# Hybrid flow backbone step on one core: the SSD's PSUM tiles in turn from two tags, and an earlier place for one part of the output projection

## The chip, the cores and the metric

The kernel runs on one core of one Trainium2 chip. The metric is device time in microseconds (us) of a whole execution; the number for a kernel is the median of its runs. PE is the matmul engine, ACT the scalar engine, DVE the vector engine, POOL the GpSimd engine, SP the engine from whose queue all DMA transfers of this kernel are issued.

## The reference, cut to what matters

Two layers work on 128 prompt tokens and 512 sample tokens of 1024 features. Each layer has a mixer with four groups of heads side by side, whose outputs are joined and projected, then a gated feed-forward net (FFN). Scales, shifts and gates come from a modulation of the conditioning vectors (adaLN).

```python
def trunk_layer(x, mod, P, layer_idx, ctx):
    h = rmsnorm(x, P['g_pre1']) * (1.0 + scale1) + shift1
    ...
    ya = diff_attention(a_q, a_k, a_v, lam)
    ...
    yb = gqa_attention(b_q, b_k, b_v).reshape(b, L, W_B)
    ...
    y = jnp.concatenate([ya, yb, yc.astype(ya.dtype), yd.astype(ya.dtype)], axis=-1) @ P['w_out']
    x = x + gate1 * rmsnorm(y, P['g_post1'])
    h = rmsnorm(x, P['g_pre2']) * (1.0 + scale2) + shift2
    ...

def ssd_scan(x, dt, A, Bm, Cm, h0):
    ...
    decay = jnp.where(mask, jnp.exp(jnp.where(mask, seg, 0.0)), 0.0)
    gmat = jnp.einsum('btlhn,btshn->btlsh', Cc, Bc) * decay
    y_diag = jnp.einsum('btlsh,btshp->btlhp', gmat, xc)
    decay_to_end = jnp.exp(a_cum[:, :, -1:, :] - a_cum)
    chunk_states = jnp.einsum('btshn,btsh,btshp->bthpn', Bc, decay_to_end, xc)
    chunk_decay = jnp.exp(a_cum[:, :, -1, :])
    ...
    y_off = jnp.einsum('btlhn,bthpn,btlh->btlhp', Cc, h_enter, jnp.exp(a_cum))
    return (y_diag + y_off).reshape(b, L, h, p), h_final
```

The mixer's 1024 output features are 8 chunks of 128: 0 to 3 come from the two attentions, 4 and 5 from the SSD (a state space model with scalar decays), 6 and 7 from the S5 mixer.

## The kernel before, in words

Everything is kept with features on the 128 partitions and 642 columns of tokens, split into two groups of columns (256 and 386, `SPANS`). Large matmuls run in three passes over a high and a low part of both operands (`lin3`, L124), so that each weight tile of 128x1024 is loaded (`wr`), cast on ACT to its high part (`wh`, L103) and subtracted on DVE or POOL in turn to its low part (`wl`, L106). Pool `wp` holds two buffers each of `wr`, `wh` and `wl` for all streamed weights of the kernel; in layer 0 the modulation's weights (`wm`, L234) use the same two `wr` buffers.

A scheduler orders the instructions at compile time. Each instruction has a priority (lower goes first), which counts up by one per instruction from the number given to `prio(...)` (L1428); the numbers are in `PR` and `WP` (L42, L43). Each engine then executes its own list in that order, and waits in it for its operands. Tiles of one pool and tag share the tag's buffers.

PSUM has eight banks: tag p two, e two, d two, v one, u one (`pss`, L157). The projections, the head norms, the modulation of layer 0 and the output projection take p (the latter's last part p and e in turn); the S5 mixer, its gated output and the whole SSD take d; attention takes e, u and v.

The mixer (`mixer`, L1438) writes a layer's work down in this order, each part with its priority relative to the layer's base: input projections and key and query preparation (40000), the SSD's step sizes (`ssd_steps`, 55000, one p tile), the S5 mixer (0), in layer 0 modulation group 1 (`fill(0)`, 60000, two p tiles), the S5 gated output (10000), the SSD (30000), attention (35000), the output projection over chunks 6 and 7 (61000), in layer 0 modulation group 2 (`fill(1)`, 61000, two p tiles), the output projection over chunks 0 and 1 (62000; the weights' chunks are stored in the order 0, 2, 1, 3, so these are the first unit of each attention). Then come the norms (300000), with the output projection over the other four chunks for one group of columns after the other, and the FFN (320000). The first input weights of layer 1 have the priority 321000 (L470).

```python
1488              with self.pool(f"sd{l}", "right") as sd, self.prio(base + PR["ssd"]):
1489                  self.ssd(l, sd, pb)
1490              proj.close()
1491              with self.prio(base + PR["attn"]):
1492                  self.attention(l, at, kq)
1493          y = [yp.tile([P, TW], F32, tag=f"y{c}", name=f"y{c}") for c in range(8)]
1494          with self.prio(base + WP[0]):
1495              self.w_out(l, y, self.w_out_load(l, 6, 2))
1496          fill(1, base + PR["f1"])
```

A modulation group (`adaln`, L224) sums 8 input chunks into one p tile: per chunk two loads of 512 KB and four matmuls; then a second p tile brings the sums to the partitions. `w_out` (L1512) goes over 8 output tiles and the two groups of columns, 16 p tiles in all for two chunks; chunks 6 and 7 come first and are copied to y by ACT (L1525), later parts are added by DVE (L1527). In pool `wo` stand the weights of the last part; it and the tiles of x lie in the space of the SSD's pool `sd`.

The SSD (`ssd`, L928) takes its PSUM tiles in this order: six tiles of transposes (L940); eight chunk states, forward and backward (L959); then for each of five token chunks two tiles of B against C, whose product with the mask is `sd_cbm` (L985), two tiles of log decays from POOL's `sd_md` (L991) for which ACT takes the exponential (L997) and DVE the product with `sd_cbm` (L998), one tile for the inside of the chunk (`pyd`), and, but for the prompt's chunk, one of entering decays and two of entering states; the sums into y are POOL's (L1026, L1028) and DVE's (L1030). At the end come two tiles for the norm's sums of squares. Its tiles in SBUF have one buffer for each direction.

Of the kernel before, what the change touches and what calls it, by code (L numbers as in the profile page):

```python
# [14 lines left out]
P = 128  # L15
# [27 lines left out]
WP = (61000, 62000)  # L43
# [32 lines left out]
class K:  # L76
# [10 lines left out]
    def load_w(self, src, nk, nm=128, keep=None, parts=None):  # L87
        """weights as (hi, lo) with hi + lo exact; they stay in the pool `keep` if one is given"""
# [20 lines left out]
    def load_w2(self, src, pool):  # L109
        """the same for 8 input chunks, as lists of their parts, in the place of hidden chunks"""  # L110
# [13 lines left out]
    def lin3(self, o, w, xs):  # L124
        """o = w^T x in three passes over the (hi, lo) parts"""
        n = len(xs)
        for k, (xh, xl) in enumerate(xs):
            wh, wl = (t[k] if isinstance(t, list) else t[:, k] for t in w)
            self.mm(o, wh, xh, k == 0, False)
            self.mm(o, wh, xl, False, False)  # L130
            self.mm(o, wl, xh, False, k == n - 1)
# [17 lines left out]
    def tri(self, lower, strict):  # L149
        """mask of the triangle of the rows not below (or not above) the columns"""  # L150
        o = int(strict == lower)
        return self.c("lt" if lower else "su")[:, o:o + 128]
# [13 lines left out]
    # exact-ish exponential on small tiles: returns (p, s), exp(x) = s * (1 + p)  # L166
# [30 lines left out]
    def cmul(self, pool, dre, dim, ar, ai, br, bi, nm, shp, e1=None, e2=None):  # L197
        """d = a * b on float planes (broadcast APs allowed)"""
# [17 lines left out]
    # ------------------------------------------------------------ adaLN  # L216
# [7 lines left out]
    def adaln(self, l, lo, hi, pool, banks="pp", bufs=2):  # L224
        """groups lo .. hi - 1 of 2048 columns of the modulation, in steps"""
# [16 lines left out]
    def adaln_end(self, l, g, parts, ps, pool, bank, sel, bufs):  # L242
        """column sums to the features on partitions; the 512s of a group lie in the order 0, 2, 1, 3"""
# [14 lines left out]
    def adaln_first(self, pool):  # L258
        """shift and scale of the first norm, half of the features after the other"""
# [12 lines left out]
    def gains(self, l, which):  # L272
        """(1 + scale) * g_pre, gate * g_post for sub-block `which` (0 mixer, 1 FFN)"""
# [20 lines left out]
    # ------------------------------------------------------------ norms  # L294
    def rsqrt(self, pool, ss, n, feats, tag):
        """(ss / feats + EPS) ** -0.5 on a small tile"""
# [8 lines left out]
    def square(self, pool, ps, gi, src, c, n=8, tmp=None):  # L305
        """adds src ** 2 over the features of chunk c of n for one group of tokens to the sums in ps (on the rows of a
        quarter, which depends on the chunk)"""
# [7 lines left out]
    def rstd(self, pool, ps, gi, feats, tag="n", tmp=None):  # L315
        """per token 1 / rms from the sums in ps, on all partitions of ps; a function of the columns"""
# [17 lines left out]
    def prenorm(self, pool, l, which, gi, acc):  # L334
        """h = rmsnorm(x) * (1 + scale) * g_pre + shift for one group of tokens"""
# [19 lines left out]
    def postnorm(self, pool, l, which, gi, acc, y, nacc, out=None):  # L355
        """x += gate * rmsnorm(y) * g_post for one group of tokens; nacc collects the squares of the new x"""
# [18 lines left out]
    def norms(self, pool, gi, st, y, post, pre, out=None):  # L375
        """from the sums of a group of tokens to the next activations; the end of the first group comes behind the
        start of the second one"""
# [9 lines left out]
    def between(self, m):  # L387
        """the rest of the first group's norms, once output tile MID of the second group is under way"""
        if m == MID and self.pending:
            self.pending()  # L390
            self.pending = None

    # ------------------------------------------------------------ input projection tiles
    def leading(self, jobs, bank, keep, wprio, place=None):
        """several output tiles, one group of the tokens after the other;
        jobs: (weights, put(first column, PSUM)), bank(i): PSUM tile"""
# [11 lines left out]
    def put(self, d, alt=0):  # L408
        """plain evacuation to the columns of a tile"""
# [10 lines left out]
    def dwconv(self, x, w, b, out):  # L420
        """centred depthwise conv of width 3 along the token axis"""
# [6 lines left out]
    def silu2(self, t, out, half):  # L428
        """out = silu(2 * half) by way of t"""
# [3 lines left out]
    def ysplit(self, c, src, scale=None):  # L433
        """mixer output chunk c (sample columns from 0, prompt columns at the end of src) to (hi, lo)"""
# [11 lines left out]
    # ------------------------------------------------------------ S5  # L446
    def first_proj(self, l, pb, lead):
        """inputs of the S5 mixer (columns ordered by position in the chunk of 8, chunk), first queries and keys,
        gates of the SSD"""
# [24 lines left out]
    def s5_tables(self, l, pool, bank="dd", wprio=None, bufs=1):  # L474
        """tables that depend on the parameters alone, to DRAM"""
# [17 lines left out]
        # step sizes, a_bar, input gain  # L493
# [56 lines left out]
        # powers a^0..a^8  # L550
# [6 lines left out]
        # unit phases e^{i theta 8 2^s}, decay |a|^8  # L557
# [13 lines left out]
        # powers per position in the chunk: into the states, out of the states  # L571
# [11 lines left out]
        for qt in range(4):  # L583
# [4 lines left out]
            # B_bar (with one group of zero padding)  # L588
# [13 lines left out]
            # state-in table, transposed to rows (channel, position)  # L602
# [21 lines left out]
            # state-out table  # L624
# [17 lines left out]
            # kernels between taps: columns tau = -7..7  # L642
# [21 lines left out]
            # rotation tables over chunk index (sample 64 | prompt 16)  # L664
# [3 lines left out]
            # decay with segment starts cleared  # L668
# [18 lines left out]
    def s5(self, l, pool, pb):  # L687
# [16 lines left out]
        # tokens to (channel, position) rows  # L704
# [8 lines left out]
        for qt in range(4):  # L713
# [11 lines left out]
            # chunk inputs to the states  # L725
# [9 lines left out]
            # rotated inputs, decayed sums, states entering each chunk  # L735
# [28 lines left out]
            # outputs in rows (channel, position), in the place of the inputs  # L764
# [9 lines left out]
            # back to rows of channels  # L774
# [4 lines left out]
            # gelu (tanh form) of y + d * u, twice its value  # L779
# [17 lines left out]
    def s5_glu(self, l, pool, ys):  # L797
        """gated output (its input is twice the gelu)"""
# [21 lines left out]
    # ------------------------------------------------------------ token-major V | dt  # L820
# [21 lines left out]
    # ------------------------------------------------------------ SSD  # L842
# [13 lines left out]
    def ssd_steps(self, pj):  # L856
        """step sizes and decays"""
# [22 lines left out]
        # token-major, order (dir, chunk, head)  # L880
# [40 lines left out]
        # chunk decay per (group, state) row: [dir, chunk, hh]  # L921
# [6 lines left out]
    def ssd(self, l, pool, pj):  # L928
# [4 lines left out]
        # token-major x, B  # L933
        xt = pool.tile([P, 5, 256], F32, tag="sd_xt", name="sd_xt")
        bt = pj.tile([P, TW], F32, tag="raw", name="sd_bt", bufs=2)[:, 0:640].rearrange("p (a b) -> p a b", b=128)
        for src, dst in ((xf[0], xt[:, :, 0:128]), (xf[1], xt[:, :, 128:256]), (bfm, bt)):
            for ta, tb in ((0, 3), (3, 5)):
                pb = self.pss("d")
# [10 lines left out]
        # chunk states (transposed: rows (group, state), columns (hh, p)) and their recurrence  # L949
# [8 lines left out]
        for di, t in order:  # L958
            ps = self.pss("d")  # L959
# [13 lines left out]
        # per chunk outputs  # L973
# [3 lines left out]
        for t in range(5):  # L977
            c0 = CH[t]
            pcb = [self.pss("d") for _ in range(2)]
# [7 lines left out]
            for di in range(2):  # L987
# [5 lines left out]
                pd = self.pss("d")  # L993
# [8 lines left out]
            pyd = self.pss("d")  # L1002
# [6 lines left out]
            if t < 4:  # L1009
                pea = self.pss("d")  # L1010
# [8 lines left out]
                for c in range(2):  # L1019
                    pyo = self.pss("d")  # L1020
# [11 lines left out]
        # gate, norm over the 256 channels  # L1032
        for c in range(2):
            V.tensor_mul(y[c], y[c], self.cz[c])
        for gi, (t0, t1) in enumerate(SPANS):
            ps = self.pss("d")
# [10 lines left out]
    # ------------------------------------------------------------ attention  # L1047
# [4 lines left out]
    def rope(self, pool, x, out):  # L1052
        """out = rotated x (sample columns)"""
# [9 lines left out]
    def headnorm(self, pool, sq, bank, tag):  # L1063
        """1 / rms over the 64 features of each of two heads, token-major [128, (token tile, head)]"""
# [5 lines left out]
    def headscale(self, rq, bank):  # L1070
        """the same on the rows of the heads; yields (columns, PSUM) for sample and prompt"""
# [19 lines left out]
    def qk_prep(self, l, pool, name, raw):  # L1091
        """projected queries or keys -> (norm) -> rope -> (hi, lo)"""
# [26 lines left out]
    def attn_unit(self, l, pool, kq, kind, u, aa=0):  # L1119
        """two score maps: kind 0 the maps aa of two differential heads, kind 1 two query heads sharing one key head"""  # L1120
# [221 lines left out]
    # ------------------------------------------------------------ FFN  # L1342
    def ffn_first(self, l, pool, yp):
        """the first output tiles of the up projection"""
# [432 lines left out]
```

## Time and profile before

| | us |
|---|---|
| median of 3 runs | 2281.47 |
| lowest, highest | 2275.59, 2284.01 |
| span of the profiled execution | 2270.7 |
| PE busy | 2064.1 (91%) |
| DVE busy | 1166.1 (51%) |
| ACT busy | 728.5 (32%) |
| POOL busy | 706.0 (31%) |

The page gives the profiled execution's span, from its first to its last instruction; its whole time is not listed, and the median of the runs is 10.8 us above this span. Busy times are sums over an engine; a matmul's duration overlaps the next one's, so that a busy PE is not PE at its peak. Layer 0 runs to about 1150, layer 1 from there. The output projection ends at about 635 in layer 0 and 1742 in layer 1.

### The profile page before, as it was taken

The page shows a single profiled execution, that of the slowest core. Times are in us where ns is not written, and L with a number is a line of the kernel's source. Part 1 is how long each engine was busy: PE and PEld are TensorE (multiplying, and loading weights), DVE is VectorE, ACT ScalarE, POOL GpSimd, SP SyncE. Part 2 cuts the span into 40 slices and gives each one's busy share as a digit, 9 for nine tenths or more (in the row PEclk, how much of TensorE's full clock was granted, in tenths as well). Part 3 has the DMA queues.
Part 4 walks back from the last instruction along what each step waited for, and adds up shares of the span by engine and source line. Part 5 has one row for each costly group of instructions (what it writes and reads, how often), then busy time and mean ns, then how long its engine had stood idle before and what let it go on. Part 6 is the DMA issues. An engine that isn't in the chain of part 4 may idle for free.

```text
span 2270.7 us, 32188 instructions
## 1 busy us (share of the span) xinstructions
PE 2064.1 (91%) x12698; PEld 1692.5 (75%) x12698; DVE 1166.1 (51%) x2376; ACT 728.5 (32%) x1256; POOL 706.0 (31%) x747
## 2 busy tenths in 40 slices
PE   5994988899999999999988889887989999999997
PEld 2884753454779788899976877655557899999985
DVE  7864874434558567233335358564565451323343
ACT  3421342232344223223324224343234443323231
POOL 4642523222232344122223324322233231212131
PEclk9996988889999999999998989888988999999998
DMA  7554324314313575422222542321022012222221
GB/s 285 165 179 135 121 68 124 93 49 142 108 38 108 166 247 186 131 82 63 84 77 77 174 131 90 111 67 49 11 65 94 19 47 84 70 80 68 82 75 47
DMA packets 95199, 232.19 MB, mean 102 GB/s; under 512 B 18120, under 2 KB 31816, under 8 KB 95048
## 3 DMA queue, kind: packets, MB, share of 16 engines
q1 hardware_dynamic: 95048, 230.14, 32.0%
q8 instruction: 100, 1.64, 0.3%
q14 instruction: 51, 0.42, 0.1%
HBM read 193.52 MB, written 36.58 MB: 101 GB/s over the span
## 4 chain that ended last, share of the span: by engine, by line
PE 75%; DMA 9%; DVE 7%; POOL 3%; issue 2%; ACT 2%; SPq 2%; POOLq 0%; DVEq 0%; ACTq 0%
PE psb L85 34%; PE psp L85 14%; PE pse L85 9%; PE psv L85 7%; PE psd L85 7%; PE psu L85 2%; DMA wm<-in_w_mod 1%; DMA ck<-in_cache_bk 1%; DMA ck<-in_cache_ak 1%; DMA wr<-in_w_down 1%; DMA s5yd<-s_u 1%; DMA wr<-in_w_out 1%; DMA s_tb<-s5td 1%; DMA s_u<-s5ud 1%; SPq L1160 1%
## 5 line engine op out<-in xcount | busy, mean ns | idle before, releaser
L85 PE MATMUL psb<-hh,wh 128*128 128x256 f32 (+1 forms) x1152 | 358.9, 312 | 2.3 <-DVE cv L425 2.3
L85 PE MATMUL psb<-hl,wh 128*128 128x256 f32 (+1 forms) x1152 | 357.9, 311 | 0.0
L85 PE MATMUL psb<-hh,wl 128*128 128x256 f32 (+1 forms) x1152 | 357.0, 310 | 0.0
L106 POOL TENSOR_TENSOR wl<-wr,wh 128x1024 fp32r<-128x1024 f32 (+3 forms) x83 | 181.6, 2188 | 449.5 <-ACT wh L103 427.1
L103 ACT CAST wh<-wr 128x1024 fp32r<-128x1024 f32 (+3 forms) x166 | 160.4, 966 | 427.9 <-PE psb L85 285.1
L85 PEld LDWEIGHTS psb<-hh,wh 128*128 128x128 f32 x1152 | 217.8, 189 | 13.2 <-issue 8.2
L85 PEld LDWEIGHTS psb<-hl,wh 128*128 128x128 f32 x1152 | 218.5, 190 | 3.4 <-issue 3.4
L85 PEld LDWEIGHTS psb<-hh,wl 128*128 128x128 f32 x1152 | 217.8, 189 | 3.4 <-issue 3.4
L85 PE MATMUL psp<-hh,wh 128*128 128x386 f32 (+1 forms) x544 | 182.2, 335 | 40.2 <-DVE dtr L839 13.1
L106 DVE TENSOR_TENSOR wl<-wr,wh 128x1024 fp32r<-128x1024 f32 (+3 forms) x83 | 95.2, 1147 | 184.5 <-ACT wh L103 184.0
L85 PE MATMUL psp<-hl,wh 128*128 128x386 f32 (+1 forms) x544 | 176.3, 324 | 1.5 <-DVE hl L353 1.4
L85 PE MATMUL psp<-hh,wl 128*128 128x256 f32 (+1 forms) x544 | 175.6, 324 | 0.0
L85 PE MATMUL psb<-uh,wh 128*128 128x256 f32 (+1 forms) x544 | 169.7, 312 | 0.0
L85 PE MATMUL psb<-ul,wh 128*128 128x256 f32 (+1 forms) x544 | 168.9, 310 | 0.0
L85 PE MATMUL psb<-uh,wl 128*128 128x256 f32 (+1 forms) x544 | 168.6, 310 | 0.0
L85 PEld LDWEIGHTS psp<-hh,wh 128*128 128x128 f32 x544 | 109.7, 202 | 52.8 <-DVE dtr L839 13.6
L85 PE MATMUL psv<-at_e,vt 128*64 128x512 f32 x240 | 136.3, 681 | 10.2 <-ACT at_e L1237 10.1
L1377 POOL TENSOR_TENSOR cv<-cv,cv 128x642 f32<-128x642 f32 x44 | 71.3, 1622 | 169.6 <-DVE cv L425 140.2
L85 PE MATMUL pse<-k,q 96*128 96x128 f32 (+5 forms) x288 | 100.2, 407 | 21.9 <-issue 6.7
L424 DVE SCALAR_TENSOR_TENSOR cv<-psb,vec,cv 128x641 f32<-128x641 f32 x72 | 63.4, 881 | 103.3 <-ACT cv L423 103.3
L85 PEld LDWEIGHTS pse<-k,q 96*128 96x128 f32 (+2 forms) x288 | 54.4, 205 | 79.0 <-issue 59.6
L85 PEld LDWEIGHTS psp<-hl,wh 128*128 128x128 f32 x544 | 109.5, 201 | 4.0 <-DVE hl L353 2.5
(497 smaller groups left out, 4596.5 us busy)
## 6 DMA issues: line engine op xcount, KB each, us to landing
wm<-in_w_mod SPq DMA_DIRECT2D x96, 512.0 KB
wr<-in_w_up SPq DMA_DIRECT2D x88, 512.0 KB
wr<-in_w_in SPq DMA_DIRECT2D x30, 512.0 KB
wr<-in_w_down SPq DMA_DIRECT2D x32, 384.0 KB
wr<-in_w_down SPq DMA_DIRECT2D x32, 320.0 KB
wr<-in_w_out SPq DMA_DIRECT2D x16, 512.0 KB
s_tb<-s5td SPq DMA_DIRECT2D x8, 992.0 KB
s_to<-s5td SPq DMA_DIRECT2D x8, 768.0 KB
```

Of the source, the lines that this page charges most:

```text
L85: self.nc.tensor.matmul(out, w, x, start=start, stop=stop)
L103: nc.scalar.copy(hv, rv)
L106: e.tensor_sub(lv, rv, hv.bitcast(F32))
L424: nc.vector.scalar_tensor_tensor(out[:, 1:TW], x[:, 0:TW - 1], w[:, 0:1], out[:, 1:TW], op0=ALU.mult, op1=ALU.add)
L1160: nc.sync.dma_start(k2[0:64, 0:TW].bitcast(F32), self.qd["bk"][0, r])
L1377: G.tensor_mul(cv[0], cv[0], cv[1])
```

## The change

The SSD takes its PSUM tiles from d and p in turn, in the order in which it asks for them. The output projection over chunks 6 and 7 is written down ahead of the SSD instead of behind attention, with the priority 20000 in place of 61000. Doc strings and comments also go; the rest of the diff is this.

```diff
-WP = (61000, 62000)
+WP = (20000, 62000)
...
     def ssd(self, l, pool, pj):
...
+        bank = itertools.cycle("dp")
...
-                pb = self.pss("d")
+                pb = self.pss(next(bank))
...
-            ps = self.pss("d")
+            ps = self.pss(next(bank))
             xe = scaled(we, di, t, "xd")
...
-            pcb = [self.pss("d") for _ in range(2)]
+            pcb = [self.pss(next(bank)) for _ in range(2)]
...
-                pd = self.pss("d")
+                pd = self.pss(next(bank))
...
-            pyd = self.pss("d")
+            pyd = self.pss(next(bank))
...
-                pea = self.pss("d")
+                pea = self.pss(next(bank))
...
-                    pyo = self.pss("d")
+                    pyo = self.pss(next(bank))
...
-            ps = self.pss("d")
+            ps = self.pss(next(bank))
             for c in range(2):
                 self.square(pool, ps, gi, y[c], c, 2, (f"sd_ex{c}", 512, 1))
...
             yp = self.right.enter_context(self.pool(f"y{l}", "right"))
+            y = [yp.tile([P, TW], F32, tag=f"y{c}", name=f"y{c}") for c in range(8)]
+            with self.prio(base + WP[0]):
+                self.w_out(l, y, self.w_out_load(l, 6, 2))
             with self.pool(f"sd{l}", "right") as sd, self.prio(base + PR["ssd"]):
                 self.ssd(l, sd, pb)
             proj.close()
             with self.prio(base + PR["attn"]):
                 self.attention(l, at, kq)
-        y = [yp.tile([P, TW], F32, tag=f"y{c}", name=f"y{c}") for c in range(8)]
-        with self.prio(base + WP[0]):
-            self.w_out(l, y, self.w_out_load(l, 6, 2))
         fill(1, base + PR["f1"])
```

## Rows read from the trace of the kernel before

**Rows 1.** The page: span of the profiled execution.
```profile
span 2270.7 us, 32188 instructions
```

**Rows 2.** Table of stretches: length, PE, PEld, DVE, ACT, POOL busy, granted clock, DMA, GB/s.
```profile
480.00:556.00 76.00, 70.76 (x276) 28.92 (x276) 29.02 (x53) 17.64 (x38) 10.21 (x13) 0.84 0.35 104
1566.00:1681.00 115.00, 108.25 (x602) 67.95 (x601) 63.74 (x113) 33.99 (x69) 38.86 (x42) 0.97 0.07 20
1681.00:1708.00 27.00, 19.80 (x94) 15.94 (x93) 16.32 (x24) 9.46 (x18) 6.70 (x4) 0.62 0.41 132
```

**Rows 3.** Timeline of PE, layer 0: start, us, instruction, count [idle before <-releaser].
```profile
348.93 1.44 PE L85 MATMUL psp<-sd_small,cst 128*128 128x20 f32 x6
350.30 1.08 PE L85 MATMUL psp<-wm,sc 128*32 128x512 f32 x4
...
411.02 1.05 PE L85 MATMUL psp<-wm,sc 128*32 128x512 f32 x4
...
438.89 0.58 PE L85 MATMUL psp<-hh,wh 128*128 128x256 f32 x1 [8.19 <-ACT wh L103]
...
482.54 1.93 PE L85 MATMUL psp<-wm,sc 128*32 128x512 f32 x8 [4.80 <-ACT y L1525]
...
552.33 0.60 PE L85 MATMUL psp<-wm,sc 128*32 128x512 f32 x2
...
557.84 0.38 PE L85 MATMUL psp<-hh,wh 128*128 128x256 f32 x1
...
589.18 0.39 PE L85 MATMUL pse<-hh,kh 128*128 128x256 f32 x1 [0.71 <-DVE at_rec L1254]
...
634.28 0.81 PE L85 MATMUL psd<-nsq,cst 128*32 128x386 f32 x2
```

**Rows 4.** Timeline of SP's queue, layer 0: second weight load of modulation group 1.
```profile
276.74 0.33 SPq L234 DMA_DIRECT2D wm<-in_w_mod  x1
```

**Rows 5.** Timeline of SP's queue, layer 0, 410 to 427.
```profile
410.31 0.70 SPq L1142 DMA_DIRECT2D q<-d_aq  x1
...
424.15 2.40 SPq L96 DMA_DIRECT2D wr<-in_w_out  x2
```

**Rows 6.** Timeline of SP's queue, end of layer 0's FFN.
```profile
1145.16 5.64 SPq L96 DMA_DIRECT2D wr<-in_w_down  x3
1151.42 11.62 SPq L96 DMA_DIRECT2D wr<-in_w_in  x4
```

**Rows 7.** Table of stretches, PE alone: tag d in layer 0, tag p in layer 1.
```profile
335.00:589.00 254.00, 46.50 (x351) 0.88 0.35 107
...
1490.00:1692.00 202.00, 37.41 (x204) 0.89 0.13 40
```

**Rows 8.** Timeline of PE: first state and first chunk (layer 0), two later chunks (layer 1).
```profile
366.51 0.66 PE L85 MATMUL psd<-sd_xd,sd_bt 128*64 128x128 f32 x8
...
387.10 0.49 PE L85 MATMUL psd<-cf,cf 64*128 64x128 f32 x4
...
1649.04 0.48 PE L85 MATMUL psd<-cf,cf 64*128 64x128 f32 x2
...
1667.76 0.49 PE L85 MATMUL psd<-cf,cf 64*128 64x128 f32 x2
```

**Rows 9.** Timeline of PE, layer 1: step-size sums, the projection behind them, its last part.
```profile
1524.34 0.81 PE L85 MATMUL psp<-sd_small,cst 128*128 128x20 f32 x6
1524.98 0.37 PE L85 MATMUL psp<-hh,wh 128*128 128x256 f32 x1
...
1692.53 0.58 PE L85 MATMUL psp<-hh,kh 128*128 128x256 f32 x1 [3.09 <-ACT kh L103]
```

**Rows 10.** Waits of PE in layer 1, 1380 to 1760: us in total, times, longest.
```profile
PE psp L85 <- ACT y L1525: 11.6, 1, 11.6
```

## The prediction

> **What bounds the kernel now.** I began with the page: PE carries the kernel, and the question is what PE does in the stretch of each layer that the change touches, from the end of the S5 mixer to the end of the output projection. The table of stretches shows it nearly always at work there: 70.76 of 76 us between 480 and 556, 108.25 of 115 us between 1566 and 1681 [rows 2]. PE loses time in two ways only: idle gaps, and the lower of its two clock levels (a mean grant of 0.84 to 0.97 in those two stretches). So a reordering can gain no more than these gaps and this clock, and it loses whatever PE work ends up behind a wait with nothing beside it.
>
> The timeline of PE then shows which order the work around the change keeps. Follow the tiles of tag p (two banks) in layer 0 [rows 3]: the SSD's step-size sums at 348.93, modulation group 1 from 350.30 to 412.1, the S5 chunks' output projection from 438.89 until 477.7 (482.54 less its wait of 4.80), modulation group 2 from 482.54 to 552.9, the projection over the first two chunks from 557.84, the rest of it from 589.18 to 635.1. One follows the other and never overlaps it. This is the order in which the code asks for the tiles, not the order of priorities or of readiness: group 1's second weight tile was asked for at 276.74 [rows 4], and its first matmul ran 74 us later, directly behind the step-size sums. Weights show the same: the first weights of layer 1 have priority 321000, ahead of most of layer 0's FFN (from 320000 on, one per instruction), and were still issued only after the last w_down load [rows 6]. I therefore read each tag as a queue in program order. In layer 0 the p queue is as long as the attention beside it: both end at about 589.
>
> **The change, part by part.**
>
> *SSD tiles move into the p queue.* The SSD asks for 51 tiles (6 transposes, 8 states, 32 in four chunks, 5 in the last chunk), then 2 for its norm; every second one now comes from p. By the reading above these stand behind group 1 and behind the S5 chunks' projection, and group 2 (layer 0) and the first two chunks' projection (both layers) stand behind the SSD's last p tile, that of its first norm group. Until now they ran beside the SSD.
>
> *Layer 0, the sum along the p queue.* Group 1 still ends at 412.1, since the step sizes and the modulation weights before it do not change. The projection's weights wait in the raw-weight queue behind group 1's sixteen tiles; SP issued them at 424.15, behind attention loads that began at 410.31 [rows 5]. At the new priority they may go as the slot comes free, at 412; with the 14.7 us that lay between issue and first matmul (424.15 to 438.89) that gives 427. Ends: 427 and 439; I take 427. The two weight loads pass attention's loads on SP, which cost that queue under 2.4 us (the issue row of both), beside work of other units: nothing. The projection itself: layer 1's p work, 37.41 us for two such projections, gives 18.7 each [rows 7]; end 446. Upper end 38.8, as it took between attention work before. Its 16 copies on ACT and two casts go ahead of attention's exponentials, but they existed before, so PE's total is unchanged.
>
> Then the SSD. Its states took 20.6 us with two banks (366.51 to 387.10) [rows 8]; with four, and three transposes left to do, I take 18. A chunk took 18.7 us with two banks where no DMA disturbed it (1649.04 to 1667.76) [rows 8], and 23 on average in layer 1 (115 for five [rows 2]). Below, PE's own SSD work is a bound: 46.50 us in all [rows 7], 9.3 a chunk. More banks cannot remove the chain mask product, matmul, exponential, product, matmul, sum, nor its single buffers outside PSUM. I take 15, nearer to 18.7, because every step of that chain waits in a queue that attention uses too. So 18 + 75 + 5 up to the norm's squares = 98, ends 61 (12 + 46.5 + 3) and 141 (21 + 115 + 5). That puts group 2's start at 544, against 482.54.
>
> Group 2: 62 us for group 1 and 70 for itself before; I take 60, since its first pair of weights is there and attention is nearly over. End 604. The next projection begins 5 us later (552.9 to 557.84), takes 18.7, and the rest of the output projection 46 (589.18 to 635.1) less 4 of overlap: 609 + 18.7 + 42 = 670, against 635. **Layer 0: +34 us** (-3 with the lower SSD end alone, +77 with the upper one).
>
> What covered group 2 so far was attention and the SSD. That cover is gone: attention, relieved of the SSD between 366 and 446, ends early, and PE has only group 2's few matmuls while SP and PE hand two raw-weight slots back and forth.
>
> *Layer 1* has no modulation groups. The projection starts, as before, behind the step-size sums at 1524.34 [rows 9]. The SSD's p transposes and its states wait for it, some 15 us, which the faster chunks (15 against 23) give back more than once. The gain is at the end: the projection over the remaining chunks began at 1692.53 after 3.09 us for its weights [rows 9], since their place is the SSD's, and the stretch 1681 to 1708 has 19.80 us of PE work at a mean grant of 0.62 [rows 2]. With the weights there, the 7 idle us go, and some 7 of the slow clock. The first chunks' projection fills PE at attention's end instead of earlier: nothing. The wait of 11.6 us for ACT [rows 10] stays, because ACT stood behind a key load of attention that nothing here moves. **Layer 1: -13 us**, ends -22 and +12 (the delay of the SSD's start not made good).
>
> The sum is +21 on the profiled execution's span, 2270.7 [rows 1], so 2291.7; the median of the runs lies 10.8 above that span (the page gives no total for that execution), so I say 2302.
>
> Two rules stand beside this. The Trainium skill (Perfetto Trace Analysis, Optimization Strategy) says that a kernel whose most-contended engine changes over time may gain by interleaving its regimes. That speaks against this change: group 2, a DMA-paced regime, ran interleaved at 70.76 busy us of 76, and is taken out of it. The Trainium skill (Perfetto Trace Analysis, Matmuls) also has independent matmul groups rotate through different PSUM banks, so that one is emptied while the next is filled. By it the sum would be that of the first rival below, 2266; the 18.7 us of a chunk with two banks, twice PE's share of 9.3, agree with it so far.
>
> **The rivals.**
> *The SSD becomes short.* If four banks let a chunk run at PE's own 9 to 10 us, the SSD takes some 61 to 65, the p queue ends no later than before, and layer 1's 13 us remain: 2281.5 - 3 - 13 = 2266. It decides at an SSD length of 77 us, below which the sum is negative; below 66 it is a gain that can be measured. For it: a chunk has eight tiles and two banks, and 18.7 is about twice PE's share. Against it: the same chain crosses ACT, DVE and POOL. Chance 0.20.
> *The queue is not in program order.* Then SSD tiles take p whenever it is free, group 2 stays where it was, the waits of 8.19 and 4.80 for the projection's weights and copies [rows 3] go, and layer 1 gains as above: 2281.5 - 13 - 13 = 2256. Rows 3, 4 and 6 speak against it. Chance 0.06. In this case alone the projection really runs ahead by priority; by my reading layer 0 gets most of its new place from the queue.
> *It evens out.* An SSD of 66 to 88 us makes layer 0's loss about as large as layer 1's gain: 2281. Chance 0.20.
>
> **How the numbers follow.** The forecast, layer 0's longer p queue, has 0.50, and 0.04 more goes to worse outcomes of the same sign (attention's loads set back by the new order). A measurement of this kernel can tell about 0.5% from no change, 11.4 us. Faster: 0.20 + 0.06 = 0.26; same 0.20; slower 0.54. The forecast's own range is 2293 to 2350. The range for 8 in 10 reaches down over the short SSD to 2262 and up to 2345, an SSD of some 125 us with layer 1 at -8.
>
> **What the changed profile would show.** Right: in layer 0, SSD transposes into p only after the S5 chunks' projection; a first matmul of group 2 at 520 to 580 instead of 482.54; PE idle on modulation weights after attention; the last sums of the output projection at 655 to 690 instead of 635. In layer 1, SSD chunks of 12 to 17 us and no wait for weights at the start of the last projection part. Wrong: SSD tiles in p before 420, or group 2 starting before 510, or chunks still 18 us and more in layer 1.

## The result, and the profile after

The changed kernel takes 2303.43 us (median of 4 runs, 2293.27 to 2304.54) against 2280.09 us of the kernel before in the same comparison: a ratio of 1.0097, 95% interval 1.0079 to 1.0115. It is slower by 23 us, and the forecast of 2302 us lies 1.4 us from the median. The page of the changed kernel begins so (the span; then each engine's busy time, its share and its instructions):

```profile
span 2302.7 us, 32209 instructions
...
PE 2085.1 (91%) x12698; PEld 1699.4 (74%) x12698; DVE 1157.2 (50%) x2376; ACT 728.6 (32%) x1256; POOL 703.4 (31%) x747
```

The span is 32.0 us longer than before [rows 1], PE's busy time 21 us (2085.1 against 2064.1), while DVE and POOL are busy for less than before. The medians differ by 23 us only, so up to 9 us of what lies between the two profiles is scatter from one execution to the next, not the change. PE's timeline of layer 0, with the tiles of tag p that answer to [rows 3] (start, us, instruction, count, idle before and its releaser):

```profile
429.62 0.58 PE L85 MATMUL psp<-hh,wh 128*128 128x256 f32 x1 [13.92 <-ACT wh L103]
...
463.71 0.38 PE L941 MATMUL psp<-identr,cf 128*128 128x128 f32 x2
...
487.12 0.49 PE L85 MATMUL psp<-cf,cf 64*128 64x128 f32 x2
...
548.02 0.40 PE L85 MATMUL psp<-nsq,cst 128*32 128x256 f32 x1
548.03 0.63 PE L85 MATMUL psp<-wm,sc 128*32 128x512 f32 x3
...
598.30 1.88 PE L85 MATMUL psp<-cst,wmt 128*128 128x8 f32 x8 [0.69 <-ACT wmt L247]
...
602.51 0.58 PE L85 MATMUL psp<-hh,wh 128*128 128x256 f32 x1 [2.33 <-ACT wh L103]
...
664.68 0.81 PE L85 MATMUL psd<-nsq,cst 128*32 128x386 f32 x2
```

The users of p stand in one row: the S5 chunks' projection from 429.62, the SSD's first transposes in p at 463.71, its norm's squares at 548.02, and 0.01 us behind them modulation group 2, which began at 482.54 before. The last squares of the output projection end at 665.5 instead of 635.1 [rows 3]: 30.4 us, which then stay (PE's instructions of layer 0's FFN stand 31 to 32 us later).

How 30 us come out of the same work is seen in the tables of stretches (length, busy PE, PEld, DVE, ACT, POOL, granted clock, DMA share, GB/s). Of the kernel before, the part beside modulation group 1 and the whole stretch of layer 0:

```profile
335.00:430.00 95.00, 84.13 (x408) 39.18 (x407) 46.36 (x99) 25.54 (x54) 31.34 (x38) 0.86 0.40 114
...
335.00:635.00 300.00, 271.54 (x1335) 150.75 (x1334) 143.91 (x260) 90.63 (x184) 80.64 (x82) 0.90 0.32 98
```

The same two of the changed kernel, with group 2 between them:

```profile
337.00:430.00 93.00, 70.71 (x264) 27.35 (x262) 34.68 (x71) 19.90 (x42) 16.21 (x18) 0.79 0.41 116
...
548.00:600.00 52.00, 36.75 (x127) 9.62 (x126) 10.35 (x19) 7.03 (x16) 3.85 (x4) 0.70 0.63 197
...
337.00:667.00 330.00, 281.42 (x1346) 153.72 (x1344) 137.26 (x262) 90.94 (x185) 81.89 (x83) 0.86 0.30 90
```

PE is idle for 48.6 us (330 less 281.4) instead of 28.5, and its busy time is 9.9 us longer at a mean grant of 0.86 instead of 0.90. Busy time times grant is nearly the same in both (242 and 244 us), so I read this as 20 us of idle time and 10 us of clock. Two places show it. Beside group 1, PE gets 264 matmuls done instead of 408, since most of the SSD's are missing there; beside group 2 there are 127 in 52 us, where the kernel before had 276 in 76 [rows 2].

Beside group 1 it is not the waits for modulation weights that grew. Group 1's matmuls among the groups of instructions (busy us, mean ns of one | idle us before them and what ended it), before and after:

```profile
L85 PE MATMUL psp<-wm,sc 128*32 128x512 f32 x64 | 18.1, 743 | 6.9 <-DMA wm<-in_w_mod 6.9
```

```profile
L85 PE MATMUL psp<-wm,sc 128*32 128x512 f32 x64 | 20.3, 783 | 7.1 <-DMA wm<-in_w_mod 7.1
```

Group 1 took 62 us with the SSD's matmuls beside it (350.30 to 412.1) and 59 without most of them (352.41 to 411.6). What is new is how long PE stands behind it: from 415.7 on it has nothing to do for 13.92 us, until the projection's weights are there (first line of the timeline above). ACT waits for them with it, and in its list attention's next exponentials come behind their cast:

```profile
428.52 1.04 ACT L103 CAST wh<-wr 128x1024 fp32r<-128x1024 f32 x1 [15.18 <-DMA wr<-in_w_out]
```

Before, ACT waited nearly as long (13.4 us up to 437.8), but four of attention's exponentials and one of the SSD's came ahead of it. So PE worked on attention and the SSD's second chunk until 430.7, and 8.19 us of idle time were left [rows 3].

In layer 1, the projection's last part no longer waits for its weights. The stretch that holds its start, which answers to 1681 to 1708 in [rows 2] (19.80 us of 27, grant 0.62), of the changed kernel:

```profile
1700.00:1725.00 25.00, 24.37 (x119) 14.73 (x118) 14.09 (x26) 9.29 (x19) 7.80 (x6) 1.00 0.22 61
```

Yet layer 1 gives back only some 2 us in all. The step-size sums begin 41.4 us later than before (1565.78 against 1524.34 [rows 9]), though layer 0 handed over 32; 11 of them are then won back by the end of the output projection.

### The profile page after: what moved, and what is told of

Same layout as the page of the kernel before. It is cut to its first block, busy times and chain, and to the rows that moved or that the text cites. A ratio compares the mean times of both kernels' runs of the same rounds, so it can differ in the third digit from the quotient of the medians.

```text
span 2302.7 us, 32209 instructions
## 1 busy us (share of the span) xinstructions
PE 2085.1 (91%) x12698; PEld 1699.4 (74%) x12698; DVE 1157.2 (50%) x2376; ACT 728.6 (32%) x1256; POOL 703.4 (31%) x747
## 4 chain that ended last, share of the span: by engine, by line
PE 73%; DMA 11%; DVE 8%; ACT 2%; POOL 2%; issue 2%; SPq 2%; POOLq 0%; DVEq 0%; ACTq 0%
PE psb L85 34%; PE psp L85 15%; PE pse L85 9%; PE psv L85 7%; PE psd L85 6%; DMA wm<-in_w_mod 2%; PE psu L85 2%; DMA s5yd<-s_u 1%; DMA wr<-in_w_out 1%; DMA ck<-in_cache_bk 1%; DMA wr<-in_w_down 1%; DMA s_tb<-s5td 1%; DMA s_u<-s5ud 1%; ACT wh L103 1%; DMA wr<-in_w_up 0%
```

## The experiments

All ten are cut from the changed kernel. Times are medians, with the ratio to the kernel before in the same comparison. The last three columns are read from one profiled execution of each: the end of the last squares of layer 0's output projection; layer 1 from the last matmul of layer 0's FFN to the step-size sums; and from there to the last squares of layer 1 in tag u. (PE ends layer 0's FFN at 1207.4 in the kernel before; the 1150 above is where SP turns to layer 1's weights.) In brackets stands how much of PE's order in that first part of layer 1 is the order of the kernel before: the share of matmuls in matching sequence, of which the low values are rough, since they depend on how matmuls are told apart.

| kernel | us | ratio (95%) | layer 0's last squares | FFN to step sums (same order) | step sums to squares |
|---|---|---|---|---|---|
| before | 2276 to 2281 | 1 | 635.1 | 316.9 | 220.2 |
| changed | 2303.4 | 1.0097 (1.0079 to 1.0115) | 665.5 | 327.3 (0.78) | 208.9 |
| banks alone | 2305.0 | 1.0113 (1.0089 to 1.0137) | 661.5 | 332.4 (0.42) | 210.2 |
| move alone | 2267.7 | 0.9938 (0.9915 to 0.9962) | 631.8 | 321.9 (1.00) | 207.5 |
| turn in layer 1 alone | 2259.2 | 0.9893 (0.9870 to 0.9915) | 635.5 | 318.7 (0.99) | 205.0 |
| turn in layer 0 alone | 2329.3 | 1.0205 (1.0178 to 1.0231) | 672.8 | 346.7 (0.77) | 206.9 |
| banks, priority, old place | 2290.5 | one run | 665.9 | 324.7 (0.35) | 205.2 |
| group 2 ahead of SSD | 2313.2 | 1.0137 (1.0115 to 1.0159) | 661.9 | 331.9 (0.42) | 217.7 |
| group 2 with eight buffers | 2288.4 | 1.0039 (1.0023 to 1.0055) | 649.8 | 323.1 (0.35) | 215.8 |
| turn in layer 1, later projection | 2259.9 | 0.9907 (0.9887 to 0.9927) | 627.9 | 318.0 (0.99) | 209.3 |
| turn in states alone (layer 0) | 2272.3 | 0.9997 (0.9974 to 1.0021) | 645.5 | 330.4 (0.78) | 204.1 |
| turn in chunks alone (layer 0) | 2284.9 | 1.0044 (1.0015 to 1.0073) | 653.7 | 321.5 (0.99) | 206.6 |

Kernels with the same text for layer 0 differ by up to 7 us in the first of these columns (changed and turn in layer 0: 665.5 and 672.8), so a few us there mean nothing. Part of this stands ahead of all that the experiments change: layer 0's step-size sums begin between 347.6 and 353.7 in the twelve profiles.

**Which half of the change costs: banks or move.** The banks alone, and below it the move alone:

```diff
-WP = (20000, 62000)
+WP = (61000, 62000)
...
-            with self.prio(base + WP[0]):
-                self.w_out(l, y, self.w_out_load(l, 6, 2))
             with self.pool(f"sd{l}", "right") as sd, self.prio(base + PR["ssd"]):
...
                 self.attention(l, at, kq)
+        with self.prio(base + WP[0]):
+            self.w_out(l, y, self.w_out_load(l, 6, 2))
```

```diff
-        bank = itertools.cycle("dp")
+        bank = itertools.cycle("d")
```

> Only the banks: SSD takes d and p in turn, the S5 chunks' projection stays behind attention in the program. If p serves its tiles in program order (theory), the order on p is group 1, SSD, projection, group 2, w_out(0,2): SSD's first p tile right behind group 1 (about 413), SSD done near 498 (84.5 us long as in the changed kernel), then the projection (19 to 35 us), group 2 from 517 to 533 instead of 548.5, so 15 to 32 us are won back of the changed kernel's 32 in layer 0: 2272 to 2295, and group 2 is still idle on its weights behind SSD. If the cost is the projection's new place and not the banks (rival): at or under the time before, 2265 to 2280, with group 2 starting near 483.

> Only the move: the projection over the S5 chunks ahead of SSD, which takes d alone. Theory (queue of p in program order): p's order is that of the kernel before, group 2 starts within 15 us of 483, the time is within 8 us of before (2272 to 2288), and layer 1's last part no longer waits for its weights. Rival (the move is the cost): +15 to +32, 2295 to 2312, SSD in layer 0 delayed by the projection's 19 to 35 us.

The banks carry the loss, and the move by itself is a gain (2267.7, below the range that I gave it). PE's timeline of the kernel with the banks alone:

```profile
408.98 0.42 PE L941 MATMUL psp<-identr,cf 128*128 128x128 f32 x2
...
516.53 0.62 PE L85 MATMUL psp<-nsq,cst 128*32 128x256 f32 x2
517.08 0.38 PE L85 MATMUL psp<-hh,wh 128*128 128x256 f32 x1
```

The order is the expected one: the SSD directly behind group 1, the projection directly behind the SSD's norm. But SSD and projection were longer than I had put in. The SSD took 108 us (408.98 to 516.53) instead of 84.5, the projection some 32, so group 2 came at 552 and not at 517 to 533, and 2305.0 is outside the range. Both the projection and group 2 now lie behind the SSD. In the kernel with the move alone, p keeps its old order, and group 2 starts 10 us earlier than before:

```profile
472.93 1.06 PE L85 MATMUL psp<-wm,sc 128*32 128x512 f32 x8
```

**Priority or place in the program.** Banks and the priority of 20000, but the call left behind attention:

```diff
-            with self.prio(base + WP[0]):
-                self.w_out(l, y, self.w_out_load(l, 6, 2))
             with self.pool(f"sd{l}", "right") as sd, self.prio(base + PR["ssd"]):
...
                 self.attention(l, at, kq)
+        with self.prio(base + WP[0]):
+            self.w_out(l, y, self.w_out_load(l, 6, 2))
```

> The changed kernel's banks and its priority of 20000, but the call of the projection over the S5 chunks left behind attention in the program. If p serves tiles in the order in which the program asks for them (theory): as with the banks alone, the projection's first matmul comes only after SSD's norm (515 or later, in spite of the higher priority), group 2 from about 550, 2295 to 2315. If priority decides who gets the tile (rival): the projection's first matmul near 430 and SSD's first p tile behind it, as in the changed kernel.

PE's timeline of this kernel, at the projection's first matmul:

```profile
521.25 0.62 PE L85 MATMUL psp<-nsq,cst 128*32 128x256 f32 x2
521.80 0.38 PE L85 MATMUL psp<-hh,wh 128*128 128x256 f32 x1
```

With a priority ahead of the SSD's, the projection still waits for the SSD's norm, as it did at 61000. In this kernel the place in the program sets who gets a tile; the priority does not. (One run, and its 2290.5 is below the 2295 I gave: layer 1 went faster, layer 0 lost the same 30.8 us.)

**Which layer.** In the first kernel the SSD turns in layer 1 alone, in the second in layer 0 alone:

```diff
-        bank = itertools.cycle("dp")
+        bank = itertools.cycle("dp" if l else "d")
```

```diff
-        bank = itertools.cycle("dp")
+        bank = itertools.cycle("d" if l else "dp")
```

> The changed kernel, but SSD takes its banks in turn in layer 1 alone, where there is no modulation group to cover it. Theory: layer 0 is as in the move alone (within 8 us of before), layer 1 is as in the changed kernel (2 us under before, up to 11 from the step sizes on): 2268 to 2285. Rival (the loss is spread over both layers): about half of the loss stays, 2288 to 2297.

> The complement: SSD takes its banks in turn in layer 0 alone. Theory: the whole loss of 32 us of layer 0 stays and layer 1's 2 us are not won: 2300 to 2315, group 2 of layer 0 from about 548. Rival (loss spread): 2288 to 2297.

Turning in layer 1 alone beats both kernels, at 0.9893 of the time before, 9 us under the range that I gave it: layer 0 is where it was (635.5), and layer 1 is 13 us shorter. By the medians, which need no profile, the turn in layer 0 on top of this costs 44 us (2303.4 against 2259.2). Turning in layer 0 alone is worse than the whole change, and worse than I expected: PE's instructions stand 38.5 us later in layer 0's FFN and 55.4 in layer 1's, so 17 come in layer 1, whose text is that of the move alone, where layer 1 was 7 us shorter than before. The table shows where: the part of layer 1 ahead of the step-size sums took 346.7 us instead of 321.9. PE's order of matmuls there is another one, though no step of it was changed. In the five kernels that keep the order of before there (0.99 and 1.00, before itself among them) this part took 317 to 322 us; in the seven where it differs, 323 to 347. That layer 0's turn alters the order further on is seen (with the turn in the states alone, below, but not in the chunks alone); how it does was not tried, and that the order makes the length is not shown: at about the same share this part took 327.3 us in the changed kernel and 346.7 in this one.

What the turn does in layer 1 is seen in the last part of its projection. The kernel with the move alone, on PE's timeline:

```profile
1679.39 0.58 PE L85 MATMUL psp<-hh,kh 128*128 128x256 f32 x1 [3.09 <-ACT kh L103]
```

And the same place with the turn in layer 1, in the table of stretches, and below it the longest of PE's waits there from the step-size sums to the last squares (total, times, longest):

```profile
1655.00:1682.00 27.00, 26.00 (x131) 15.72 (x130) 15.44 (x30) 10.81 (x22) 8.20 (x6) 1.00 0.22 66
```

```profile
PE psp L85 <- ACT y L1526: 11.2, 1, 11.2
```

Against my expectation the move alone leaves the weight wait of [rows 9] as it was; the SSD must also end earlier, so that its space is free for those weights. With the turn it does, PE has 26.00 us of work in 27 at full clock, and the wait of [rows 10] is still there. The move alone gains nearly as much here in another way: that wait of 11.6 us does not occur in it. The turn also shortens the SSD itself: the starts of its chunks in layer 1 are 14.0 us apart on the mean with it (1579.70 to 1635.64), 25.0 with the move alone and 25.4 before.

**Is it group 2 left without cover?** First, group 2 called ahead of the SSD:

```diff
+            fill(1, base + PR["f1"])
             with self.pool(f"sd{l}", "right") as sd, self.prio(base + PR["ssd"]):
                 self.ssd(l, sd, pb)
...
-        fill(1, base + PR["f1"])
```

> The changed kernel with modulation group 2 called ahead of SSD instead of behind it. Theory (each tag serves in program order, and whoever stands behind waits): p's order is group 1, projection, group 2, SSD; group 2 runs from about 466 beside attention, SSD's first p tile comes only behind it, at 525 to 545, SSD then takes 75 to 90, and SSD is what ends the stage: layer 0 later by another 15 to 35 than in the changed kernel, 2315 to 2345. Rival (what costs is only that group 2 had no work beside it): with its cover back the 32 us are won back, 2265 to 2285.

PE's timeline of this kernel, where group 2 ends, and the table of stretches:

```profile
525.47 0.39 PE L85 MATMUL psp<-cst,wmt 128*128 128x8 f32 x2
525.72 0.42 PE L941 MATMUL psp<-identr,cf 128*128 128x128 f32 x2
```

```profile
430.00:526.00 96.00, 88.27 (x336) 40.02 (x336) 35.96 (x46) 29.27 (x64) 15.24 (x13) 0.91 0.33 98
526.00:600.00 74.00, 61.53 (x395) 42.03 (x394) 39.51 (x83) 20.13 (x40) 34.67 (x42) 0.82 0.17 53
...
337.00:663.00 326.00, 281.32 (x1346) 156.72 (x1345) 141.37 (x262) 91.34 (x185) 81.07 (x83) 0.87 0.31 91
```

The order held to the microsecond: the SSD's transposes in p come between group 2's last matmuls. My size did not: the SSD, alone by then, took 66 us to its norm (525.72 to 591.04) and not 75 to 90, so 2313 is just under the range. The rival fell as well: group 2 is covered by attention again, and layer 0 ends as late as in the changed kernel (661.9). Now it is the SSD's chain that has too little beside it, 61.53 us of work in 74 at a grant of 0.82. So the order within p is not what costs, but that three stages which used to overlap stand in one row.

Then group 2 behind the SSD, as in the change, with weight buffers of its own:

```diff
-        fill(1, base + PR["f1"])
+        with self.pool(f"g2{l}", "right") as g2:
+            fill(1, base + PR["f1"], g2, 8)
```

> The changed kernel with eight weight buffers of its own for group 2, in the place of SSD's tiles, instead of the two that it shares. Theory: group 2 behind SSD is a stretch that waits for its 8.4 MB of weights, two buffers at a time; with eight it shrinks from 49 us to 36 to 42 (8.4 MB at the 236 GB/s of its densest stretch is 36 us) and the time by 7 to 13: 2288 to 2298. Rival (PE or the clock sets the stretch): group 2 stays within 3 us of 49 and the time within 4 of the changed kernel's.

Its sixteen weight loads stand side by side on SP's queue, the first issued at 545.24, the others from 568.2 on, and the stretch that follows keeps the DMA engines at 0.91:

```profile
545.24 36.12 SPq L234 DMA_DIRECT2D wm<-in_w_mod  x16
```

```profile
575.00:593.00 18.00, 15.16 (x63) 2.81 (x58) 0.00 (x0) 1.62 (x3) 0.00 (x0) 0.91 0.91 356
```

They lie in the SSD's space, and all but the first come behind the SSD's norm (555.29). Group 2's matmuls then took 24 us (568.05 to 592.01) instead of 50. Layer 0's last squares came 15.7 us earlier, more than the 7 to 13 expected, where I had reckoned with 236 GB/s and the loads reached 356; the time, 2288.4, is at the lower end of its range. The rival is out. Group 2 also began later, though: from the norm's first squares to its second tile it is 36.7 us (555.29 to 592.01) instead of 50.3 (548.02 to 598.30). So about a quarter of group 2's uncovered stretch goes with the handing back and forth of two buffers.

**Which of the SSD's tiles must stay off p.** In layer 0, in the first kernel only the transposes and states turn, in the second only the chunks and the norm:

```diff
+        bank = itertools.cycle("dp" if l else "d")
         y = xf
         for c in range(2):
```

```diff
-        bank = itertools.cycle("dp")
+        bank = itertools.cycle("dp" if l else "d")
...
+        bank = itertools.cycle("dp")
         y = xf
         for c in range(2):
```

> The changed kernel, but in layer 0 only SSD's transposes and states take d and p in turn; its chunks and its norm take d alone. SSD still starts behind the projection (its first p tile near 464), but group 2 stands only behind the states, so it starts at 485 to 500 with the chunks and attention beside it. Theory A, that of the forecast (the cost is group 2 left without cover): layer 0's last squares within 8 us of the kernel before (635 to 643). Theory B (SSD on d also filled the weight waits of group 1, and both covers count): last squares 645 to 656, half of the 30 us.

> The complement: in layer 0 the transposes and states take d alone (so they run from about 336 beside group 1), the chunks and the norm take d and p in turn. The chunks' first p tile comes behind the projection, near 462; group 2 stands behind the norm, 515 to 548. Theory A (group 2's cover is the whole cost): last squares 658 to 668, nearly the 30 us of the changed kernel. Theory B (both covers count): 645 to 656.

PE's timeline, group 2's start and the last squares with the turn in the states alone, and below it the table of stretches beside group 1 and beside group 2:

```profile
489.97 1.06 PE L85 MATMUL psp<-wm,sc 128*32 128x512 f32 x8
...
644.72 0.81 PE L85 MATMUL psd<-nsq,cst 128*32 128x386 f32 x2
```

```profile
337.00:430.00 93.00, 71.42 (x264) 27.47 (x263) 34.63 (x70) 19.30 (x40) 16.17 (x18) 0.80 0.39 115
...
490.00:560.00 70.00, 69.95 (x394) 35.71 (x394) 35.23 (x61) 20.41 (x39) 26.66 (x29) 1.00 0.41 126
```

And with the turn in the chunks alone, with the stretch beside group 1:

```profile
536.70 0.63 PE L85 MATMUL psp<-wm,sc 128*32 128x512 f32 x3
...
652.91 0.81 PE L85 MATMUL psd<-nsq,cst 128*32 128x386 f32 x2
```

```profile
335.00:428.00 93.00, 70.68 (x298) 28.81 (x296) 37.53 (x82) 21.03 (x44) 21.91 (x26) 0.83 0.40 117
```

The first costs layer 0 10.4 us, though group 2 is fully covered in it (PE is busy 69.95 of 70 us from 490 to 560). What is left of the loss is that the SSD starts late: from 337 to 430 PE has the changed kernel's 264 matmuls. The second costs 18.6 us, with group 2 behind the norm as in the changed kernel. But it does not show group 2's cover by itself: its chunks wait for p until the projection is through (first p tile at 462.17), and beside group 1 PE is no busier than in the changed kernel (70.68 against 70.71 of 93 us). That the two figures make 29.0 of the 30.4 us is therefore no proof of a split. What the runs do show is the changed kernel against the first of these two: with the chunks and the norm off p, and group 2 beside them, 20.0 of the 30.4 us are gone, and 10.4 stay. Theory A, the forecast's, is refuted as the whole cause: both places count, as theory B says.

The split is rough. The kernel before and the three that make the move without the turn in layer 0 end between 627.9 and 635.5, so 645.5 lies above all four, by 10 to 18 us.

**The best version once more,** with the projection's priority behind attention's:

```diff
-WP = (20000, 62000)
+WP = (36000, 62000)
...
-        bank = itertools.cycle("dp")
+        bank = itertools.cycle("dp" if l else "d")
```

> Turns in layer 1 alone, as in the run that beat the kernel before, with the projection's priority behind attention's (36000 instead of 20000). If the projection ahead of SSD only fills gaps (theory): within 5 us of that run's 2259. If SSD's p tiles in layer 1 are held up by a projection that comes later (rival): SSD's first p tile behind 1585 instead of 1573, and 2264 to 2280.

2259.9 against 2259.2: no difference. The SSD's first p tile in layer 1 came at 1564, no later than in the other. Where the tiles of p are asked for decides here too.

## Why the prediction was right, and where it was not

*The p queue is served in program order.* Right, and it carried the sign: three kernels with three orders of calls showed these orders on PE. The second rival fell with it.

*The sum of layer 0.* +34 forecast, +30.4 measured, out of terms that were off in both directions. Group 1 ended within 2 us of its 412.1, and the first matmul of the projection came at 429.6 (forecast 427). The projection was mis-sized: it ended at 464 (34.5 us, near the upper end of 38.8 that I had set aside for 18.7 from layer 1). The SSD took 84.3 us behind it, not 98: from the first chunk's product at 474.06 to the norm's squares at 548.02 it took 74, for which I had 80, and transposes and states ahead of it cost 10 rather than 18, since the last states ran beside the first chunk. Group 2 began at 548.0 (544), took 50 and not 60. The end came at 665.5 (670).

*Where the loss comes from.* The step that says what covered group 2 is right for about two thirds (20.0 of 30.4 us go with that cover). The step that costs the move of the SSD's tiles has a gap: it says that they stand behind group 1, but not what PE loses there. The other third, 10.4 us, stays with the SSD's late start alone. It is not that the SSD had filled group 1's waits for weights, as theory B has it: these were 6.9 us and are 7.1. Its matmuls ran beside group 1 within the same 60 us or so, and behind group 1 PE now stands still for 13.92 us where it was 8.19: the SSD's second chunk is missing there, and the casts that go ahead of attention's exponentials, put at nothing in the sum, hold up attention too. How the 10.4 us divide between these, no run shows.

*Layer 1.* -13 was forecast from the step-size sums to the end of the projection, and that stretch shrank by 11.3 us (220.2 to 208.9), over all kernels by 2.5 to 16. Its reason held: no weight wait, a grant of 1.00 instead of 0.62. The step that failed is the silent one that all ahead of those sums stays: it grew by 10.4 us (316.9 to 327.3), in another order of the same instructions; why is open. The chunks did not get as short as said: their starts from 1607.84 to 1679.07 are 17.8 us apart on the mean, where 12 to 17 was forecast, 18 was to be a sign of being wrong, and 25.4 was the pace before by the same measure. With the turn in layer 1 alone, whose text for layer 1 is the same, they are 14.0 apart, as forecast.

*From span to median.* I added 10.8 us as if it lay around every execution. The changed kernel's profiled execution took 2304.54 us for a span of 2302.7, so 1.8. By the same 1.8 us the profiled execution of before took about 2272.5 (an estimate, since its time is not listed) and was 8 to 9 us faster than its median. This error and the missing gain in layer 1 cancel: the spans differ by 32.0 us, not 21, and the medians by 23. That the forecast came within 1.4 us is luck; its terms were off by more.

*The rivals.* The first needed an SSD under 77 us; it took 84.3, and 108 with the banks alone. By the length of the SSD the third, 66 to 88 us, would have been the one to come true. It did not because the projection ahead of the SSD was 16 us longer than I had it, and because layer 1's 13 us came only where layer 0 did not turn. So the forecast's side was right by less than its working says. The two rules each hold in a part. What the Trainium skill (Perfetto Trace Analysis, Optimization Strategy) says of interleaving regimes agrees with layer 0: group 2 ran in PE's 70.76 busy us of 76 [rows 2] before, and in 36.75 of 52 after. What the Trainium skill (Perfetto Trace Analysis, Matmuls) says of rotating PSUM banks agrees with layer 1, where the chunks' starts moved from 25.4 us apart to 17.8, and to 14.0 with the turn in layer 1 alone, and where no modulation group stands behind the SSD in the same banks.

## What to carry to other kernels

Before a stage gets a second set of PSUM banks, list who else asks for those banks, in program order: it will wait for all ahead of it and hold up all behind it, whatever the priorities say. Work that runs beside a DMA-paced stage can be worth more there than if it were faster by itself, so count what it covers at both ends of its move: beside the stage that it leaves behind, and beside the stage that now stands alone. Try a change of this kind by layer: here the same line lost some 30 us in layer 0, where modulation groups share the banks, and gained some 8 in layer 1, where none does (2267.7 with the move alone to 2259.2; the two intervals just touch).

## What was not expected of the hardware

With eight buffers instead of two the same weight loads ran at 356 GB/s and a DMA share of 0.91, against 236 GB/s and 0.74 (the loads of x among them) in the middle of group 2 in the changed kernel:

```profile
556.00:589.00 33.00, 21.27 (x74) 5.03 (x72) 9.50 (x17) 2.98 (x8) 0.85 (x1) 0.70 0.74 236
```

The other is the clock's share. Of the 30 us lost in layer 0, 10 are no waits but nearly the same matmuls (1346 against 1335 in the traces) at a lower mean grant, 0.86 instead of 0.90: it was 0.70 where PE waited for weights, and 1.00, the upper level throughout, where the SSD and attention lay beside group 2 (490 to 560 with the turn in the states alone).
